# Gate-up with three of eight pairs as seven products, and two sets of sums made again in the down stage

## The chip, the cores and the metric

The kernel runs on one core of a Trainium2 chip. The metric is the device time of one execution in microseconds, as the median of the runs. PE is the matmul engine (PEld its weight loads), DVE the vector engine, ACT the scalar engine, SP the engine that issues the weights' transfers.

## The reference

One layer of a bidirectional encoder on 256 tokens of width 2048, all in float32: a gated feed-forward block, a mixer (a gated recurrence beside windowed attention), and a second gated feed-forward block, each between two RMS norms. The change is in the two feed-forward blocks (FFN):

```python
def swiglu(x, w_gate_up, w_down):
    gate, up = jnp.split(x @ w_gate_up, 2, axis=-1)
    return (jax.nn.silu(gate) * up) @ w_down

ff = swiglu(rms_norm(x, pre_norm_ffn1[layer]), w_ffn1_gate_up[layer], w_ffn1_down[layer])
x = x + 0.5 * rms_norm(ff, post_norm_ffn1[layer])
```

w_gate_up is 2048 x 11264, w_down 5632 x 2048.

## The kernel before

**Products.** A float32 product is made as three: each operand is split into a high part h and a low part l, and h x h, h x l and l x h are added up in PSUM (three, L433 is its matmul). ACT casts the high part and DVE subtracts it from the source for the low part (split_act, L176 and L177). The activations stay on chip with both parts, xt for gate-up and ht for down; the weights are read from memory once, 1 MB at a time, into one of three raw buffers, split in halves of 128 x 1024 and used at once. Five h and five l buffers go round.

**Groups and pairs.** Gate-up runs over 11 groups of 512 gate and 512 up columns. A group has eight pairs of 128-row slices of the inner dimension, and collects 2 x 2 blocks c[m][n] of 128 x 512 in four PSUM banks (m: half of the tokens, n: gate or up). A plain pair takes 2 x 2 x 2 blocks by three products, 24 matmuls. A pair in MIXED_IN takes the seven products of a Strassen-like scheme by three, 21 matmuls (seven). For it DVE forms sums of weight blocks in place in raw (L465, L469, L471) and splits one block of 512 and three halves of 1024, against two halves for a plain pair. Four of the seven products also need sums of the activations: in gate-up these are made once per FFN, while group 0 runs (even), so group 0 is plain. Three are added straight into c, four go to the banks p, which fold adds into c once, in the pair after next from the last seven (L505 to L513); the pairs just around it have their products sorted by bank.

At a group's end, units takes silu(gate) x up out of c (L901 on ACT, L902 on DVE), and after the next group's first pair eight PE transposes (L913) bring the result into two ht tiles. For every second tile up to 18 (MIXED) sums_of then makes the sums (L390, L393, L394), which the down stage uses for its own seven-product pairs.

**Down.** Two runs (Pairs) over 22 ht tiles in the order of a written list, each for 1024 columns. left_sums splits the sums into sp; for tiles in keep it does so once and holds them for the second run. Here begin_next loads and half-splits the plain pair behind a seven ahead of its turn (AHEAD).

A scheduler of the programming layer orders the instructions of each engine when the kernel is built; each engine then runs its list in that order.

Of the kernel before, what the change touches and what calls it, by code (L numbers as in the profile page):

```python
# [11 lines left out]
F32 = mybir.dt.float32  # L12
# [5 lines left out]
ALU = mybir.AluOpType  # L18
# [19 lines left out]
def hymba_layer_kernel(  # L38
# [346 lines left out]

    S3, S1, S2, S4 = range(4)

    def sums_of(u, w):

        nc.vector.tensor_tensor(  # L390
            w[:, 0:2, :], u[:, 0, :].rearrange("p (m t) -> p m t", m=2), u[:, :, P:T], ALU.subtract
        )
        nc.vector.tensor_tensor(w[:, S2, :], w[:, S1, :], u[:, 0, 0:P], ALU.subtract)  # L393
        nc.vector.tensor_tensor(w[:, S4, :], u[:, 1, 0:P], w[:, S2, :], ALU.add)  # L394
        return w

    class Blocks:
# [3 lines left out]

        AHEAD = False
        ahead = None
# [118 lines left out]
        def work(self, upto):  # L522

            while self.pos < upto:
                u = self.order[self.pos]
                if u in self.sums:
                    v = self.order[self.pos + 1]
                    if self.AHEAD and v not in self.sums and self.pos + 1 < upto:
                        self.ahead = [v]
                        self.seven(u, self.begin_next)  # L530
                    else:
                        self.seven(u)
                else:
                    if self.ahead:
                        _, raw, h, l = self.ahead
                        self.ahead = None
                        hs, ls = zip((h, l), split_half(raw, 1))
                    else:
                        hs, ls = split_load(self.source(u))
                    if self.pos == self.after + 1:  # L540
                        self.fold()
                    places = [(k, m, n) for k in range(2) for m in range(2) for n in range(2)]
                    if self.pos in (self.after, self.after + 1):

                        places.sort(key=lambda at: at[1:])
                    for k, m, n in places:
                        self.plain(u, hs, ls, m, n, k)
                self.pos += 1

    class Pairs(Blocks):  # L550
# [4 lines left out]
        HELD = 2  # L555
        AHEAD = True

# [43 lines left out]
        def folded(self):  # L601
            if self.now == 0:
                wide = self.room.tile([P, 2, 512], F32, tag="sp", name=nm("y"), bufs=2)
                y = [
# [198 lines left out]

    MIXED_IN = (2, 4)
    MIXED = range(0, 20, 2)

    def pair_of(xt, u):
# [46 lines left out]
    def ffn(gated, w_dn, post_gain, again, gain=None, lead=None, aside=None):  # L854

        with ExitStack() as st:
# [10 lines left out]
            def sums_room(u):  # L867
                n = MIXED.index(u)
                if n == 0:
                    where_X_was.append(xp.tile([P, 8, 4, P], F32, tag="X", name=nm("sums")))  # L870
                if n < 8:
                    return where_X_was[0][:, n]
                return work.tile([P, 4, P], F32, tag=f"su{n}", name=nm("su"))

            def even(u):
# [5 lines left out]
                if u in MIXED_IN:  # L881
# [3 lines left out]
                    ws = sums_of(whole, room_for("s").rearrange("p (j t) -> p j t", j=4))  # L885
                    w = work.tile([P, 4, 2, P], F32R, tag="sp", name=nm("xs"), bufs=2)
                    split_act(w[:, :, 0, :], w[:, :, 1, :], ws)
# [8 lines left out]
            def units(c, scale):  # L896
# [10 lines left out]
                for j in range(2):  # L907
# [9 lines left out]
                    u = bank.rearrange("p (k t) -> p k t", k=2)  # L917
                    if g in MIXED:
                        u = room_for("z").rearrange("p (k t) -> p k t", k=2)
# [4 lines left out]
                    hts.append(ht)  # L924
                    if g in MIXED:
                        sums[g] = sums_of(u, sums_room(g))
# [26 lines left out]
            ]  # L953
            rows = Pairs(w_dn, orders, hts, sums, work, post_gain, keep=(10, 12, 16))
            rows.half_gain(far["pool"])
            rows.work(1)
            next(waiting)
            rows.first_run()
            rows.work(NU - 4)
# [586 lines left out]
```

## Time and profile before

| | |
|---|---|
| median of 3 runs | 1846.0 us (1845.7 to 1846.99) |
| the profiled execution | 1846.26 us, its span 1844.0 us |
| granted PE clock, mean | 0.998 |
| busy: PE, PEld, DVE, ACT | 99%, 83%, 85%, 59% |
| matmuls | 8670 |
| read from memory | 360 MB, 198 GB/s |

A row of a list of waits has the engine and line that waited, what it waited for, the total in us, how often, and the longest. A row of a timeline has the start in us, how long it took, engine, line, operation, what it writes and reads, shape, count, and in brackets the idle time before it. A row of stretches has the stretch, its length, then each engine's busy us with its count of instructions (PE, PEld, DVE, ACT, POOL), the granted PE clock, the share of time that the DMA engines were busy, and GB/s. A matmul's shown length is that of its whole passage; what it costs is the distance between starts.

### The profile page before, as it was taken

The numbers are of one execution on the slowest core, as the hardware profiler recorded it, in microseconds if no ns is written. First come the engines' busy times: TensorE is split into PE (matmuls) and PEld (weight loads), VectorE is DVE, ScalarE is ACT, GpSimd is POOL, SyncE is SP. The second block draws the span as 40 slices with busy tenths as digits, with TensorE's granted clock in tenths as the row PEclk, the third lists the DMA queues.
The fourth block names the chain that finished last, engine by engine and source line by source line (L and its number), as shares of the span: only waits on it lengthen the run. The fifth ranks groups of instructions, "written<-read, shape, count | busy, mean of one in ns | idle before, by whom it ended". The sixth has DMA issues, their size and how long they took to land.

```text
span 1844.0 us, 23256 instructions
## 1 busy us (share of the span) xinstructions
PE 1832.5 (99%) x8670; PEld 1532.8 (83%) x8670; DVE 1559.4 (85%) x1956; ACT 1078.7 (59%) x1429; POOL 21.4 (1%) x39
## 2 busy tenths in 40 slices
PE   9999999999999999999999999999999999999998
PEld 7888888888888888888888888888888888888886
DVE  7988888888999998477787788888888788899997
ACT  7555555555665666477667656455555555566563
POOL 1000000000000000000000000000000000000000
PEclk9999999999999999999999999999999999999999
DMA  7665655556555565655555456555665556555564
GB/s 254 206 206 184 205 204 184 183 186 203 216 202 211 203 247 208 204 176 158 174 181 154 169 211 223 182 198 193 208 207 193 204 185 206 210 188 188 219 248 155
DMA packets 180880, 365.78 MB, mean 198 GB/s; under 512 B 9256, under 2 KB 56448, under 8 KB 180000
## 3 DMA queue, kind: packets, MB, share of 16 engines
q1 hardware_dynamic: 180416, 364.17, 57.9%
q8 instruction: 68, 1.11, 0.2%
q14 instruction: 44, 0.36, 0.1%
q0 software_dynamic: 352, 0.14, 0.0%
HBM read 360.06 MB, written 4.21 MB: 198 GB/s over the span
## 4 chain that ended last, share of the span: by engine, by line
PE 96%; DVE 1%; ACT 1%; DMA 1%; SPq 0%; issue 0%; DVEq 0%; POOL 0%; ACTq 0%; POOLq 0%
PE pa L433 41%; PE pb L433 38%; PE pa L309 7%; PE pa L314 4%; PE pa L364 1%; PE pa L362 1%; PE pa L363 1%; DMA bias<-row 1%; PE pa L913 1%; PE pb L913 1%; DVE l L177 0%; PE pb L1415 0%; PE pb L1289 0%; PE pb L1267 0%; ACT h L176 0%; PE pb L1351 0%
## 5 line engine op out<-in xcount | busy, mean ns | idle before, releaser
L176 ACT CAST h<-raw 128x1024 fp32r<-128x1024 f32 (+1 forms) x789 | 798.9, 1030 | 635.4 <-PE pb L433 368.5
L177 DVE TENSOR_TENSOR l<-raw,h 128x1024 fp32r<-128x1024 f32 (+1 forms) x789 | 924.7, 1193 | 208.8 <-ACT h L176 175.2
L433 PE MATMUL pa<-h,xt 128*128 128x512 f32 x1248 | 431.0, 391 | 0.1
L433 PE MATMUL pb<-h,xt 128*128 128x512 f32 x1168 | 407.7, 390 | 0.0
L433 PEld LDWEIGHTS pa<-h,xt 128*128 128x128 f32 x1248 | 234.3, 188 | 48.2 <-DVE xt L232 0.6
L433 PEld LDWEIGHTS pb<-h,xt 128*128 128x128 f32 x1168 | 219.3, 188 | 46.0 <-DVE xt L232 0.5
L433 PE MATMUL pa<-l,xt 128*128 128x512 f32 x624 | 243.3, 390 | 0.1
L433 PE MATMUL pb<-l,xt 128*128 128x512 f32 x584 | 227.2, 389 | 0.0
L309 PE MATMUL pa<-xt,h 128*128 128x512 f32 x672 | 164.7, 394 | 0.0
L433 PE MATMUL pb<-h,ht 128*128 128x512 f32 x464 | 162.9, 389 | 0.0
L433 PE MATMUL pa<-h,ht 128*128 128x512 f32 x464 | 162.8, 389 | 0.0
L309 PEld LDWEIGHTS pa<-xt,h 128*128 128x128 f32 x672 | 123.0, 188 | 23.6
L433 PEld LDWEIGHTS pa<-l,xt 128*128 128x128 f32 x624 | 117.3, 188 | 24.3 <-DVE l L177 0.9
L433 PEld LDWEIGHTS pb<-l,xt 128*128 128x128 f32 x584 | 109.7, 188 | 22.6
L465 DVE TENSOR_TENSOR raw<-raw 128x1024 f32<-128x1024 f32 x84 | 102.9, 1224 | 2.2
L433 PEld LDWEIGHTS pb<-h,ht 128*128 128x128 f32 x464 | 87.1, 188 | 18.1
L433 PEld LDWEIGHTS pa<-h,ht 128*128 128x128 f32 x464 | 87.1, 188 | 18.0
L314 PE MATMUL pa<-xt,l 128*128 128x256 f32 x672 | 91.5, 285 | 0.0
L433 PE MATMUL pa<-l,ht 128*128 128x512 f32 x232 | 90.3, 389 | 0.0
L433 PE MATMUL pb<-l,ht 128*128 128x512 f32 x232 | 90.3, 389 | 0.0
L314 PEld LDWEIGHTS pa<-xt,l 128*128 128x128 f32 x672 | 87.1, 191 | 3.2
L433 PE MATMUL pa<-h,sp 128*128 128x512 f32 x176 | 61.3, 389 | 0.0
(280 smaller groups left out, 2134.5 us busy)
## 6 DMA issues: line engine op xcount, KB each, us to landing
raw<-in_w_ffn_gate_up_dram SPq DMA_DIRECT2D x350, 512.0 KB, 4.8
raw<-in_w_ffn_down_dram SPq DMA_DIRECT2D x88, 1024.0 KB, 4.9
raw<-in_w_mix_in_dram SPq DMA_DIRECT2D x52, 1024.0 KB, 5.1
raw<-in_w_mix_out_dram SPq DMA_DIRECT2D x16, 1024.0 KB, 5.3
pg<-in_post_norm_ffn_dram SPq DMA_DIRECT2D x4, 512.0 KB, 5.9
X<-in_x_dram SPq DMA_DIRECT2D x2, 1024.0 KB, 6.9
bias<-row SPq DMA_DIRECT2D x16, 128.0 KB, 4.8
kept<-X SPq DMA_DIRECT2D x2, 1024.0 KB, 4.6
```

What stands on the lines that cost most here:

```text
L176: nc.scalar.copy(hi, src)
L177: nc.vector.tensor_tensor(lo, src, hi.bitcast(F32), ALU.subtract)
L309: nc.tensor.matmul(slot[f], weights(hs, kk, f), xcol(xt, k), start=(k == 0), stop=(k == KT - 1))
L314: nc.tensor.matmul(slot[f][:, 0:T], weights(ls, kk, f), xcol(xt, kh * 8 + kk, 0), start=False, stop=False,)
L362: nc.tensor.matmul(dst, xh, h[:, o : o + n], start=(k == 0), stop=False)
L363: nc.tensor.matmul(dst, xh, l[:, o : o + n], start=False, stop=False)
L364: nc.tensor.matmul(dst, xl, h[:, o : o + n], start=False, stop=(k == KT - 1))
L433: nc.tensor.matmul(self.bank(at), lhs, rhs, start=(n == 1), stop=n in (ends, self.of[at]), skip_group_check=n > ends,)
L465: nc.vector.tensor_tensor(four[:, 0:2], four[:, 0::3], four[:, 1:2].to_broadcast([P, 2, 512]), ALU.add)
L913: nc.tensor.transpose(bank[:, o : o + P], zs[m][:, k * P : (k + 1) * P], ident)
```

## The change

MIXED_IN goes from (2, 4) to (2, 3, 5), so that three pairs of each of the groups 1 to 10 take seven products. The sums of ht tiles 16 and 18 are no longer made in gate-up and kept in tiles of their own; sums_again makes them from ht at the start of down, in another pool, and the freed room holds the third set of gate-up's sums. keep goes from (10, 12, 16) to (16, 18). The flag AHEAD goes: a seven in Gated, too, takes begin_next where its condition holds. The order of the four sums in their tile changes with it (S1 to S4). Lines behind it shift: L465 becomes L464, L902 becomes L913, L506 to L513 become L505 to L512.

```diff
-    S3, S1, S2, S4 = range(4)
+    S2, S3, S4, S1 = range(4)
...
-            w[:, 0:2, :], u[:, 0, :].rearrange("p (m t) -> p m t", m=2), u[:, :, P:T], ALU.subtract
+            w[:, S3::2, :], u[:, 0, :].rearrange("p (m t) -> p m t", m=2), u[:, :, P:T], ALU.subtract
...
                 if u in self.sums:
                     v = self.order[self.pos + 1]
-                    if self.AHEAD and v not in self.sums and self.pos + 1 < upto:
+                    if v not in self.sums and self.pos + 1 < upto:
                         self.ahead = [v]
                         self.seven(u, self.begin_next)
...
-    MIXED_IN = (2, 4)
+    MIXED_IN = (2, 3, 5)
     MIXED = range(0, 20, 2)
+    MIXED_EARLY = MIXED[:8]
...
-                if n < 8:
-                    return where_X_was[0][:, n]
-                return work.tile([P, 4, P], F32, tag=f"su{n}", name=nm("su"))
+                return where_X_was[0][:, n]
+
+            def sums_again(u):
+
+                ht = hts[u].bitcast(F32)
+                w = far["pool"].tile([P, 4, P], F32, tag=f"su{u}", name=nm("su"), bufs=1)
+                nc.vector.tensor_tensor(
+                    w.rearrange("p (k m) t -> p k (m t)", k=2), ht[:, :, 0, :], ht[:, :, 1, :], ALU.add
+                )
+                a11, a21, a12, a22 = (w[:, i, :] for i in range(4))
+                nc.vector.tensor_tensor(a22, a21, a22, ALU.subtract)
+                nc.vector.tensor_tensor(a21, a11, a21, ALU.subtract)
+                nc.vector.tensor_tensor(a11, a22, a11, ALU.subtract)
+                nc.vector.tensor_tensor(a12, a12, a11, ALU.add)
+                return w
...
-                    w = work.tile([P, 4, 2, P], F32R, tag="sp", name=nm("xs"), bufs=2)
+                    w = work.tile([P, 4, 2, P], F32R, tag="sp", name=nm("xs"), bufs=3)
...
-                    if g in MIXED:
+                    if g in MIXED_EARLY:
...
-            rows = Pairs(w_dn, orders, hts, sums, work, post_gain, keep=(10, 12, 16))
+            for u in MIXED[8:]:
+                sums[u] = None
+            rows = Pairs(w_dn, orders, hts, sums, work, post_gain, keep=MIXED[8:])
             rows.half_gain(far["pool"])
             rows.work(1)
             next(waiting)
+            for u in MIXED[8:]:
+                sums[u] = sums_again(u)
             rows.first_run()
```

The scheduler orders the engines anew. On DVE, in the middle of a group before: raw_312 is pair 2 (its last split), raw_325 pair 3, raw_330 pair 4, raw_339 pair 5.

```order
L177 TENSOR_TENSOR l_320_1773<-raw_312_1754,h_319_1772 128x1024
L177 TENSOR_TENSOR l_327_1805<-raw_325_1801,h_326_1804 128x1024
L177 TENSOR_TENSOR l_329_1809<-raw_325_1801,h_328_1808 128x1024
L177 TENSOR_TENSOR l_332_1840<-raw_330_1836,h_331_1839 128x512
L465 TENSOR_TENSOR raw_330_1836<-raw_330_1836 128x1024
L177 TENSOR_TENSOR l_334_1845<-raw_330_1836,h_333_1844 128x1024
L177 TENSOR_TENSOR l_336_1850<-raw_330_1836,h_335_1849 128x1024
L469 TENSOR_TENSOR raw_330_1836<-raw_330_1836 128x512
L471 TENSOR_TENSOR raw_330_1836<-raw_330_1836 128x512
L177 TENSOR_TENSOR l_338_1855<-raw_330_1836,h_337_1854 128x1024
L177 TENSOR_TENSOR l_341_1883<-raw_339_1879,h_340_1882 128x1024
```

The same place now: raw_327 is pair 2 (its last split), raw_340 pair 3, raw_349 pair 4, raw_354 pair 5.

```order
L177 TENSOR_TENSOR l_335_1806<-raw_327_1787,h_334_1805 128x1024
L177 TENSOR_TENSOR l_342_1838<-raw_340_1834,h_341_1837 128x512
L464 TENSOR_TENSOR raw_340_1834<-raw_340_1834 128x1024
L177 TENSOR_TENSOR l_344_1843<-raw_340_1834,h_343_1842 128x1024
L177 TENSOR_TENSOR l_346_1848<-raw_340_1834,h_345_1847 128x1024
L468 TENSOR_TENSOR raw_340_1834<-raw_340_1834 128x512
L470 TENSOR_TENSOR raw_340_1834<-raw_340_1834 128x512
L177 TENSOR_TENSOR l_348_1853<-raw_340_1834,h_347_1852 128x1024
L177 TENSOR_TENSOR l_351_1881<-raw_349_1877,h_350_1880 128x1024
L177 TENSOR_TENSOR l_353_1885<-raw_349_1877,h_352_1884 128x1024
L177 TENSOR_TENSOR l_356_1916<-raw_354_1912,h_355_1915 128x512
```

A seven now follows a seven, and the plain pair 4 stands whole behind pair 3.

On DVE at a group's end before, from the fold's addition into c[1][0]: raw_351 is pair 7, raw_362 and raw_372 are the next group's pairs 0 and 1, raw_377 its pair 2; z and s at L902 are the group's two results.

```order
L511 TENSOR_TENSOR pb_295_1661<-pb_295_1661,z_349_1925 128x512
L510 TENSOR_TENSOR pa_294_1660<-pa_294_1660,s_350_1926 128x512
L177 TENSOR_TENSOR l_355_1968<-raw_351_1960,h_354_1967 128x1024
L512 TENSOR_TENSOR s_350_1926<-pa_322_1777,z_349_1925 128x512
L177 TENSOR_TENSOR l_364_2009<-raw_362_2005,h_363_2008 128x1024
L513 TENSOR_TENSOR pb_296_1662<-pb_296_1662,s_350_1926 128x512
L177 TENSOR_TENSOR l_366_2013<-raw_362_2005,h_365_2012 128x1024
L177 TENSOR_TENSOR l_374_2065<-raw_372_2061,h_373_2064 128x1024
L177 TENSOR_TENSOR l_376_2069<-raw_372_2061,h_375_2068 128x1024
L902 SCALAR_TENSOR_TENSOR z_356_1995<-pa_294_1660,scales_111,z_356_1995 128x512
L902 SCALAR_TENSOR_TENSOR s_357_1998<-pb_296_1662,scales_111,s_357_1998 128x512
L177 TENSOR_TENSOR l_379_2100<-raw_377_2096,h_378_2099 128x512
```

Now, with raw_381, raw_391 and raw_396 as the next group's pairs 0, 1 and 2:

```order
L510 TENSOR_TENSOR pb_310_1694<-pb_310_1694,z_373_2001 128x512
L509 TENSOR_TENSOR pa_309_1693<-pa_309_1693,s_374_2002 128x512
L177 TENSOR_TENSOR l_385_2054<-raw_381_2046,h_384_2053 128x1024
L511 TENSOR_TENSOR s_374_2002<-pa_337_1810,z_373_2001 128x512
L177 TENSOR_TENSOR l_393_2106<-raw_391_2102,h_392_2105 128x1024
L512 TENSOR_TENSOR pb_311_1695<-pb_311_1695,s_374_2002 128x512
L913 SCALAR_TENSOR_TENSOR z_375_2036<-pa_309_1693,scales_111,z_375_2036 128x512
L913 SCALAR_TENSOR_TENSOR s_376_2039<-pb_311_1695,scales_111,s_376_2039 128x512
L177 TENSOR_TENSOR l_395_2110<-raw_391_2102,h_394_2109 128x1024
L177 TENSOR_TENSOR l_398_2141<-raw_396_2137,h_397_2140 128x512
```

The fold has moved from pair 6 to pair 7 of its group: it runs among the next group's splits, and its last addition (L512) stands right in front of the two results. On PE the last products of the group into c[1][1] (pb_311) follow it, behind seven products of the next group (pa_377, pa_378 and one into pb_379):

```order
L432 MATMUL pa_378_2043<-h_382_2049,xt_11_123 128x512
L432 MATMUL pb_379_2044<-h_382_2049,xt_11_123 128x512
L432 MATMUL pb_311_1695<-h_369_1993,xt_12_124 128x512
L432 MATMUL pb_311_1695<-l_370_1994,xt_12_124 128x512
L432 MATMUL pb_311_1695<-h_369_1993,xt_12_124 128x512
L432 MATMUL pb_311_1695<-h_371_1997,xt_12_124 128x512
L432 MATMUL pb_311_1695<-l_372_1998,xt_12_124 128x512
L432 MATMUL pb_311_1695<-h_371_1997,xt_12_124 128x512
L432 MATMUL pb_379_2044<-l_383_2050,xt_11_123 128x512
```

Before, they stood ahead of all of the next group's (pb_296 is c[1][1], pa_358 the next group's c[0][0]):

```order
L433 MATMUL pb_295_1661<-h_354_1967,xt_12_124 128x512
L433 MATMUL pb_296_1662<-h_354_1967,xt_12_124 128x512
L433 MATMUL pb_296_1662<-l_355_1968,xt_12_124 128x512
L433 MATMUL pb_296_1662<-h_354_1967,xt_12_124 128x512
L433 MATMUL pa_358_2001<-h_363_2008,xt_11_123 128x512
```

So the group's second result on DVE now waits for products that come later.

At the start of down DVE had, from the last group's second result on (raw_772 is the first seven of down, sp a set of sums split for it or ahead):

```order
L902 SCALAR_TENSOR_TENSOR s_749_4052<-pb_687_3715,scales_111,s_749_4052 128x512
L177 TENSOR_TENSOR la_775_4156<-raw_772_4151,ha_774_4155 128x512
L177 TENSOR_TENSOR l_777_4161<-raw_772_4151,h_776_4160 128x1024
L465 TENSOR_TENSOR raw_772_4151<-raw_772_4151 128x1024
L177 TENSOR_TENSOR sp_788_4182<-sums_109_681,sp_788_4182 128x4x128
```

and has now (ht_663 and ht_731 are tiles 16 and 18, raw_808 the plain pair in front of that seven):

```order
L913 SCALAR_TENSOR_TENSOR s_788_4129<-pb_724_3790,scales_111,s_788_4129 128x512
L876 TENSOR_TENSOR su_806_4194<-ht_663_3486 128x512
L876 TENSOR_TENSOR su_807_4200<-ht_731_3831 128x512
L880 TENSOR_TENSOR su_806_4194<-su_806_4194 128x128
L880 TENSOR_TENSOR su_807_4200<-su_807_4200 128x128
L881 TENSOR_TENSOR su_806_4194<-su_806_4194 128x128
L881 TENSOR_TENSOR su_807_4200<-su_807_4200 128x128
L882 TENSOR_TENSOR su_806_4194<-su_806_4194 128x128
L882 TENSOR_TENSOR su_807_4200<-su_807_4200 128x128
L883 TENSOR_TENSOR su_806_4194<-su_806_4194 128x128
L883 TENSOR_TENSOR su_807_4200<-su_807_4200 128x128
L177 TENSOR_TENSOR l_812_4213<-raw_808_4206,h_811_4212 128x1024
```

The ten rows of sums_again stand ahead of the second half of that plain pair and of the first seven.

More of the change, by code (lines that the diff above doesn't have):

```diff
@@ L397, in hymba_layer_kernel @@
     class Blocks:
-        AHEAD = False
         ahead = None
@@ L555, in hymba_layer_kernel @@
         HELD = 2
-        AHEAD = True
         def __init__(self, w, orders, tiles, sums, room, gain_src, keep=()):
@@ L602, in folded @@
             if self.now == 0:
-                wide = self.room.tile([P, 2, 512], F32, tag="sp", name=nm("y"), bufs=2)
+                wide = self.room.tile([P, 2, 512], F32, tag="sp", name=nm("y"), bufs=3)
                 y = [
@@ L924, in units @@
                     hts.append(ht)
-                    if g in MIXED:
+                    if g in MIXED_EARLY:
                         sums[g] = sums_of(u, sums_room(g))
```

## The prediction

> **What bounds the kernel now.** I read the page's totals first, then the list of PE's waits, then the busy time of single stretches: the end of group 0, one later gate-up group, and the start of the down stage.
>
> ```profile
> PE 1832.5 (99%) x8670; PEld 1532.8 (83%) x8670; DVE 1559.4 (85%) x1956; ACT 1078.7 (59%) x1429; POOL 21.4 (1%) x39
> ```
>
> ```profile
> PE pb L130 <- DVE idle L124: 1.4, 1, 1.4
> PE pb L1415 <- ACT pt L1407: 0.4, 1, 0.4
> PE pb L210 <- DMA X<-in_x_dram: 0.4, 1, 0.4
> PE pa L210 <- DMA X<-in_x_dram: 0.2, 1, 0.2
> ```
>
> ```profile
> 14.00:58.00 44.00, 44.00 (x207) 35.62 (x205) 39.49 (x71) 30.25 (x61) 2.71 (x5) 1.00 0.64 219
> 185.62:228.67 43.05, 43.05 (x195) 35.75 (x194) 35.77 (x42) 23.01 (x27) 0.00 (x0) 1.00 0.58 196
> 487.00:530.00 43.00, 43.00 (x195) 35.73 (x194) 42.07 (x49) 27.96 (x36) 0.00 (x0) 1.00 0.54 194
> ```
>
> The four waits of PE come to 2.4 us, and none is for a split of weights. In a group (the second stretch; the columns are its length, then the busy time of PE, PEld, DVE and ACT) PE is busy throughout at a granted clock of 1.00, while DVE is busy for 35.77 of 43.05 us and idle for 7.28. The last row says how far this can go: at the start of down DVE is busy for 42.07 of 43.00 us, 98%, and PE still waits for nothing. So PE's count of products sets the time, and DVE may come close to full before PE feels it.
>
> One product's pitch, and that of a transpose, come from PE's timeline of this group:
>
> ```profile
> 191.07 0.27 PE L913 MATMUL pa<-ident,z 128*128 128x128 f32 x1
> ...
> 191.83 0.27 PE L913 MATMUL pb<-ident,s 128*128 128x128 f32 x1
> ...
> 203.06 0.39 PE L433 MATMUL pa<-l,xt 128*128 128x512 f32 x1
> ...
> 205.10 0.39 PE L433 MATMUL pa<-l,xt 128*128 128x512 f32 x1
> ```
>
> The first two rows are the first and the last of eight transposes, 0.76 / 7 = 0.11 us apart. The last two are nine products apart: 2.04 / 9 = 0.2267 us. A group is six plain pairs of 24 products, two of 21, and the transposes: 186 x 0.2267 + 0.89 = 43.05 us, which is the stretch's length. Nothing else is on the path.
>
> **Fewer products.** In each of ten groups per FFN (group 0 stays plain) one more pair takes 21 products in place of 24: 3 x 20 = 60 products, 60 x 0.2267 = 13.6 us less. The Trainium skill ("TensorE: Matmul & The Clock Gate", section "Wait — 56ns, not 53.3ns?") gives N / 2.4 GHz + 2.5 ns for a product at full clock, 215.8 ns for 512 columns. By that the term would be 12.9 us; the trace's 0.2267 decides.
>
> **More work on DVE in a group.** Its durations, from DVE's timeline of the same group, a row of PE's, two of ACT's, and DVE's groups of instructions in this stretch:
>
> ```profile
> 185.33 0.74 DVE L902 SCALAR_TENSOR_TENSOR z<-pa,scales,z 128x512 f32<-128x512 f32 x1
> 185.99 0.74 DVE L902 SCALAR_TENSOR_TENSOR s<-pb,scales,s 128x512 f32<-128x512 f32 x1
> ...
> 201.68 1.23 DVE L465 TENSOR_TENSOR raw<-raw 128x1024 f32<-128x1024 f32 x1
> ...
> 205.24 0.68 DVE L469 TENSOR_TENSOR raw<-raw 128x512 f32<-128x512 f32 x1
> 205.96 0.69 DVE L471 TENSOR_TENSOR raw<-raw 128x512 f32<-128x512 f32 x1
> 207.84 5.82 DVE L177 TENSOR_TENSOR l<-raw,h 128x1024 fp32r<-128x1024 f32 x5 [1.19 <-ACT h L176]
> 213.58 0.69 DVE L506 TENSOR_TENSOR s<-pb,z 128x512 f32<-128x512 f32 x1
> 214.18 0.69 DVE L507 TENSOR_TENSOR pa<-pa,z 128x512 f32<-128x512 f32 x1
> ...
> 217.24 0.69 DVE L511 TENSOR_TENSOR pb<-pb,z 128x512 f32<-128x512 f32 x1
> ...
> 221.30 0.69 DVE L513 TENSOR_TENSOR pb<-pb,s 128x512 f32<-128x512 f32 x1
> ```
>
> ```profile
> 184.71 0.62 PE L433 MATMUL pb<-h,xt 128*128 128x512 f32 x2
> ```
>
> ```profile
> 185.14 0.69 ACT L901 ACTIVATE s<-pb,scales 128x512 f32<-128x512 f32 x1 [0.40 <-PE pb L433]
> ```
>
> ```profile
> 203.01 1.05 ACT L176 CAST h<-raw 128x1024 fp32r<-128x1024 f32 x1 [0.96 <-DVE raw L465]
> ```
>
> ```profile
> L390 DVE TENSOR_TENSOR sums<-z 128x256 f32<-128x256 f32 x1 | 0.4, 418 | 0.0
> L393 DVE TENSOR_TENSOR sums<-sums,z 128x128 f32<-128x128 f32 x1 | 0.3, 282 | 0.0
> ```
>
> By starts, a subtraction of 1024 takes (213.58 - 207.84) / 5 = 1.15, one of 512 takes 0.60, and 0.72 where it waits for the one before it. A seven-product pair has beyond a plain one: one subtraction of 512, one of 1024, an addition of 1024 and two of 512, so 0.60 + 1.15 + 1.15 + 0.60 + 0.60 = 4.1 us. DVE's group becomes 35.8 + 4.1 = 39.9 us of 42.4. Two casts more on ACT (1.05 + 0.6) leave it at 25 of 42 us; no transfer is added, and none moves past another on SP.
>
> The change's words speak of an interleaving. In gate-up it doesn't happen: work is called pair by pair with upto = u + 1, so self.pos + 1 < upto never holds, and DVE's order shows no row of pair 4 inside pair 3. Only down interleaves, as before.
>
> **Whether 39.9 fits into 42.4.** What counts is where DVE must wait. I follow a group by hand from E, the end of PE's last product into c[1][1], which the new order puts behind seven products of the next group.
>
> From E to its use of the low part of pair 3's last half, PE has 17 products left of pair 0, 24 of pair 1, 21 of pair 2, 17 of pair 3, and 8 transposes: 79 x 0.2267 + 0.89 = 18.8 us. DVE's L913 into s begins about 0.2 after E, as L901 does here: the product it waits for has its turn until 184.71 + 0.23 = 184.94, and it begins at 185.14. Then follow, to the same low part: that instruction 0.66; six subtractions of 1024, 6.9; two additions of 1024, the first awaited, 1.27 + 1.15; seven rows of 512, one awaited, 4.3; the three small ones of sums_of at 0.34 + 0.3 + 0.3, by the groups' rows less the overlap; and after L470 a hole, since the cast waits for it and the subtraction for the cast: 0.69 + 0.10 + 1.05 + 0.04, then 1.22. The sum is 18.4. One wait is added: five h buffers go round, and pair 3's first cast (512 wide, 0.6) needs the one that PE gives back at the end of pair 1, at E + 41 x 0.2267 + 0.89 + 0.2 = E + 10.4. Its low part can begin at E + 11.05, and DVE is there at E + 10.7: 0.35. Together 0.2 + 18.4 + 0.35 = 18.95, against 18.8: PE waits for about 0.2 us here, in every group.
>
> The fold is the second place. It now stands at pair 7, the last one. DVE reaches L505 after nine more subtractions of 1024, one of 512 and three additions (10.35 + 0.6 + 2.6), at E + 32.4; PE begins pair 6 (17 + 24 + 21 + 21 + 24 + 21 = 128 products) at E + 0.2 + 128 x 0.2267 + 0.89 = E + 30.1. The fold's rows give 217.24 + 0.69 - 213.58 = 4.35 to the addition into c[1][0] and 221.30 + 0.69 - 213.58 = 8.4 to the one into c[1][1], with one and three plain subtractions between as in the new order: E + 36.8 and E + 40.8. PE needs them 30 products (pair 6 and pair 7's into c[0][0]) and 49 after that start, at E + 36.9 and E + 41.2. Both hold, the first by 0.1. So a group is 42.37 + 0.2 = 42.6 us. Bounds of the wait: 0 (a little slack in any term) to 1.3 (one more cast of 1.05 that nothing covers, plus this 0.2). I take 0.2, the hand sum itself: 20 x 0.2 = 4.0 us.
>
> **Group 0.** It makes a third set of sums: additions of 512 and 256, two of 128, one split of 512, 0.6 + 0.34 + 0.6 + 0.6 = 2.2 us on DVE, once per FFN. The first stretch has DVE busy for 39.5 of 44, so most is covered, but group 1's two sevens follow at once. Bounds 0 and 2.2; I take 0.7, twice 1.4.
>
> **Down.** Two sets of sums are made anew behind the last L913: two additions of 512 and eight small ones in two chains, 2 x 0.6 + 8 x 0.2 = 2.8 us (by L393's full length, 282 ns, 3.5). DVE also comes there with one plain half less done, 1.15. What it has to spare:
>
> ```profile
> 487.37 0.74 DVE L902 SCALAR_TENSOR_TENSOR s<-pb,scales,s 128x512 f32<-128x512 f32 x1
> ...
> 497.44 1.22 DVE L177 TENSOR_TENSOR l<-raw,h 128x1024 fp32r<-128x1024 f32 x1
> ...
> 512.35 1.23 DVE L177 TENSOR_TENSOR l<-raw,h 128x1024 fp32r<-128x1024 f32 x1 [0.16 <-ACT h L176]
> ```
>
> The low part of down's first seven is ready at 498.7. PE reaches it 63 products and 8 transposes after about 487.1: 502.3, 3.6 later. The new order takes 2.8 + 1.15 of that and gives one split of 512 back, 0.6: about 0.3 is left. DVE has no idle time until 512.35, so the pairs behind it run with the same thin lead. Bounds 0 and 2.5 (3.5 + 1.15 - 3.6, and a hole of 1.05 with it); I take 0.7 per FFN, 1.4. In the second half of down one split more (0.6 on DVE, pairs 10 and 12 against 18) lies under PE's products; without that cover it would cost 0.6 per FFN. The sums no longer made in groups 8 and 9 only free DVE.
>
> **Sum.** -13.6 + 4.0 + 1.4 + 1.4 = -6.8. The profiled run took 1846.26 us (span 1844.0 and 2.3 around it), the median is 1846.0. Predicted: 1839.2.
>
> **The rivals.** *DVE sets gate-up's pace.* For: only 2.5 of 42.4 us remain idle on it, a hole of 1.2 at pair 3, 0.35 for a buffer and 0.95 at E (the six products behind L512, less L913 into z) already fill them, and the hole isn't covered. Against: 98% at the start of down without a wait. It decides from 43.05 - 39.9 = 3.15 us of idle per group; with one more uncovered cast a group is 43.5, 20 x 0.45 + 2.8 = +11.8, 1858; if all of today's 7.28 stayed, 47.2 and +83. The Trainium skill ("Perfetto Trace Analysis", section "Identifying the Most-Contended Engine") holds PE's matmul occupancy for no measure of its limit and ranks by weight-load share, which here would put DVE's 85% before PEld's 83% and so predict this rival; the 98% row speaks against it. Chance 0.24.
>
> *Nothing gained.* Waits of 0.5 to 0.7 per group eat the products: within 0.2% of 1846.0, about what a measurement of this kernel can tell from no change (1842.3 to 1849.7). Chance 0.13.
>
> *No wait at all.* Each of my terms is off by a few tenths in favour: -13.6 + 0 to 2.6, so 1832.4 to 1835. Were the interleaving real, pair 4's half would cover the hole and this would be the forecast; as ordered, chance 0.13.
>
> My forecast, 1835 to 1842.3, has 0.50. Slower and "nothing" both lie above it, and below it little: the range goes from 1832 to 1853, leaving out about half of the first rival. Faster 0.63, same 0.13, slower 0.24.
>
> **What would show it.** Right: the groups' stretches at 42.4 to 42.8 us with DVE busy for about 39.9; among PE's waits one for DVE's l at L177, about 0.2 in each group, with 20 to 40 entries; down's start with short waits for l. Wrong: groups at 43 or more; waits of PE for L509, L510 or L512, or for h (the fold or a buffer, not pair 3); the loss outside gate-up; a granted clock below 1.00 behind such waits.

## The result and the profile after

The changed kernel takes 1851.47 us (median of 7 runs, 1851.16 to 1853.58) against 1846.0: a ratio of 1.0032, 95% interval 1.002 to 1.0043. Forecast was 1839.2 with a range of 1832 to 1853. The time lies inside the range, which was drawn wide enough to take in half of a rival, and on the wrong side of no change. Two of the seven runs, 1853.21 and 1853.58, had a mean granted clock of 0.997, the others 0.998 or 0.999. The profiled execution took 1851.47 us with a span of 1849.2, 5.2 more than before.

The shares of the chain that ended last, before:

```profile
PE 96%; DVE 1%; ACT 1%; DMA 1%; SPq 0%; issue 0%; DVEq 0%; POOL 0%; ACTq 0%; POOLq 0%
```

The page's totals and these shares after:

```profile
PE 1829.1 (99%) x8610; PEld 1518.2 (82%) x8610; DVE 1637.6 (89%) x2076; ACT 1102.8 (60%) x1469; POOL 21.4 (1%) x39
...
PE 77%; DVE 16%; ACT 4%; issue 2%; DMA 1%; ACTq 0%; DVEq 0%; POOL 0%; SPq 0%; POOLq 0%
```

The 60 products are gone from PE (8670 to 8610), and yet PE is shown busy for 99%, as before. The chain tells more: a sixth of the span now runs over DVE, where it was 1%. PE's waits (in total, times, longest):

```profile
PE pb L432 <- DVE l L177: 5.1, 20, 0.3
PE pb L432 <- ACT h L176: 2.3, 5, 0.7
PE pa L432 <- ACT h L176: 1.9, 2, 1.0
```

The first row has 20 entries, the number that the prediction asked for, but not where it put them: 18 are at pair 3 of groups 2 to 10, one stands at another place in the first FFN's group 1 and one in the second down stage. Two more rows, 4.2 us together, are new: casts for which PE waits in the two groups 1 and the two down stages. The prediction had named waits for h only as a sign of its being wrong. The same three stretches as before (length, busy time of PE, PEld, DVE, ACT): the end of group 0, one later group, and the start of down.

```profile
14.00:58.00 44.00, 44.00 (x206) 35.66 (x205) 39.66 (x72) 29.40 (x60) 2.72 (x5) 1.00 0.63 222
190.03:232.97 42.94, 42.69 (x193) 35.05 (x192) 39.44 (x47) 24.24 (x29) 0.00 (x0) 1.00 0.57 196
490.70:533.70 43.00, 43.00 (x194) 35.36 (x193) 43.00 (x56) 27.65 (x35) 0.00 (x0) 1.00 0.50 181
```

A group takes 42.94 where 42.6 was forecast. DVE is busy for 39.44 of it, near the 39.9 that were worked out. At the start of down DVE has no idle time left: 43.00 of 43.00, before 42.07. The granted clock is 1.00 in all three.

Where the 5.2 us arise can be read from PE's timeline. A group's result is transposed one pair into the next stage, so the first transpose of a group's result into pa marks the group's end, one pair late; these are those of groups 1 and 10 of each FFN, before:

```profile
104.96 0.27 PE L913 MATMUL pa<-ident,z 128*128 128x128 f32 x1
...
492.44 0.27 PE L913 MATMUL pa<-ident,z 128*128 128x128 f32 x1
...
1226.55 0.27 PE L913 MATMUL pa<-ident,z 128*128 128x128 f32 x1
...
1614.03 0.27 PE L913 MATMUL pa<-ident,z 128*128 128x128 f32 x1
```

and after:

```profile
107.75 0.27 PE L924 MATMUL pa<-ident,z 128*128 128x128 f32 x1
...
494.29 0.27 PE L924 MATMUL pa<-ident,z 128*128 128x128 f32 x1
...
1230.53 0.27 PE L924 MATMUL pa<-ident,z 128*128 128x128 f32 x1
...
1617.13 0.27 PE L924 MATMUL pa<-ident,z 128*128 128x128 f32 x1
```

With the spans these give five stretches. The table has the difference to before in us, for the changed kernel and for five of the experiments told below (their marks are the same transposes). The first row ends behind group 1, and "group 1 to 10" holds groups 2 to 10.

| stretch | changed | e3_two | f3_25 | f1_edges | h3_behind | f2_135 |
|---|---|---|---|---|---|---|
| start to group 1 | +2.8 | -0.1 | +0.3 | 0.0 | +0.1 | -0.2 |
| group 1 to 10, first FFN | -0.9 | 0.0 | 0.0 | +0.4 | -0.7 | -3.8 |
| down, mixer, to group 1 of the second | +2.1 | -0.4 | +2.6 | -0.3 | 0.0 | -0.4 |
| group 1 to 10, second FFN | -0.9 | 0.0 | 0.0 | +0.2 | -0.4 | -3.4 |
| second down and end | +2.1 | 0.0 | +1.0 | 0.0 | +0.4 | +0.4 |

The nine steps from group 1 to 10 should have brought 9 x 0.68 = 6.1 us by products alone and brought 0.9. Here is the place, first in PE's timeline, then in DVE's:

```profile
208.33 0.39 PE L432 MATMUL pb<-h,xt 128*128 128x512 f32 x1
208.96 0.50 PE L432 MATMUL pb<-l,xs 128*128 128x512 f32 x1 [0.25 <-DVE l L177]
209.30 0.39 PE L432 MATMUL pb<-h,xs 128*128 128x512 f32 x1
```

```profile
190.03 0.75 DVE L913 SCALAR_TENSOR_TENSOR s<-pb,scales,s 128x512 f32<-128x512 f32 x1 [1.52 <-PE pb L432]
...
200.80 0.69 DVE L177 TENSOR_TENSOR l<-raw,h 128x512 fp32r<-128x512 f32 x1 [0.48 <-ACT h L176]
...
205.79 0.69 DVE L470 TENSOR_TENSOR raw<-raw 128x512 f32<-128x512 f32 x1
207.69 5.24 DVE L177 TENSOR_TENSOR l<-raw,h 128x1024 fp32r<-128x1024 f32 x5 [1.20 <-ACT h L176]
```

It is the low part of pair 3's last half, in each of groups 2 to 10. The product comes 0.63 after the one before it instead of 0.2267, which is 0.41 late, and the next one starts 0.34 after it, another 0.11. So 0.52 us go here per group, though the list of waits shows 0.25: a product is drawn 0.39 long against a pitch of 0.2267, and what fits between the two counts as busy. On DVE stand the three idle times that the prediction named: for PE at the group's end (1.52; it said 0.95), for the buffer (0.48; it said 0.35) and for the cast behind L470 (1.20, as said).

### The profile page after: what moved, and what is told of

The parts are those of the page before. It is cut to its first block, busy times and chain, and to the rows that moved or that the text cites. A ratio compares the mean times of both kernels' runs of the same rounds, so it can differ in the third digit from the quotient of the medians.

```text
span 1849.2 us, 23410 instructions
## 1 busy us (share of the span) xinstructions
PE 1829.1 (99%) x8610; PEld 1518.2 (82%) x8610; DVE 1637.6 (89%) x2076; ACT 1102.8 (60%) x1469; POOL 21.4 (1%) x39
## 4 chain that ended last, share of the span: by engine, by line
PE 77%; DVE 16%; ACT 4%; issue 2%; DMA 1%; ACTq 0%; DVEq 0%; POOL 0%; SPq 0%; POOLq 0%
PE pa L432 29%; PE pb L432 28%; PE pa L309 8%; DVE l L177 8%; PE pa L314 4%; ACT h L176 4%; DVE raw L464 3%; DVE raw L470 2%; DVE raw L468 1%; PE pa L364 1%; PE pa L363 1%; PE pa L362 1%; DVE sp L177 1%; DVE la L177 1%; PE pa L924 0%
## 5 line engine op out<-in xcount | busy, mean ns | idle before, releaser
L176 ACT CAST h<-raw 128x1024 fp32r<-128x1024 f32 (+1 forms) x829 | 819.3, 1021 | 509.5 <-PE pb L432 149.2
L177 DVE TENSOR_TENSOR l<-raw,h 128x1024 fp32r<-128x1024 f32 (+1 forms) x829 | 955.8, 1181 | 108.5 <-ACT h L176 74.8
L432 PE MATMUL pa<-h,xt 128*128 128x512 f32 x1168 | 406.4, 392 | 0.1
L432 PE MATMUL pb<-h,xt 128*128 128x512 f32 x1048 | 368.5, 390 | 0.1
L432 PEld LDWEIGHTS pa<-h,xt 128*128 128x128 f32 x1168 | 219.3, 188 | 44.8 <-DVE xt L232 0.6
L432 PEld LDWEIGHTS pb<-h,xt 128*128 128x128 f32 x1048 | 196.8, 188 | 41.3 <-DVE xt L232 0.5
L432 PE MATMUL pa<-l,xt 128*128 128x512 f32 x584 | 227.8, 390 | 0.0
L432 PE MATMUL pb<-l,xt 128*128 128x512 f32 x524 | 204.1, 390 | 0.0
L464 DVE TENSOR_TENSOR raw<-raw 128x1024 f32<-128x1024 f32 x104 | 127.1, 1222 | 1.2
L432 PE MATMUL pb<-h,xs 128*128 128x512 f32 x240 | 84.6, 391 | 1.7 <-ACT h L176 1.7
```

The lines of the kernel that those rows point to most:

```text
L176: nc.scalar.copy(hi, src)
L177: nc.vector.tensor_tensor(lo, src, hi.bitcast(F32), ALU.subtract)
L432: nc.tensor.matmul(self.bank(at), lhs, rhs, start=(n == 1), stop=n in (ends, self.of[at]), skip_group_check=n > ends,)
L464: nc.vector.tensor_tensor(four[:, 0:2], four[:, 0::3], four[:, 1:2].to_broadcast([P, 2, 512]), ALU.add)
```

## The experiments

Each was timed in five rounds against the kernel before, on the same chip; only changed lines are shown.

**e2_interleave.**

```diff
-                    if v not in self.sums and self.pos + 1 < upto:
+                    if v not in self.sums and self.pos + 1 < max(upto, self.whole):
+        whole = KT // 2        # in Gated; 0 in Blocks
```

> Edit: in gate-up the interleaving that the change's words announce is made real, so that half a split of pair 4 stands on DVE between the last two additions of pair 3, where DVE now idles for 1.2 us. Theory 1 (a short lead: DVE's chain from the end of the old group to pair 3's last half is too long by 0.4 us, and PE loses 0.5 there in every group): the half of pair 4 is work that is only moved ahead, the hole stays as long for PE or is filled with 1.15 of other work, so PE's wait at pair 3 stays or grows a little unless the cast was what DVE waited for; if the filled hole doesn't delay the last half, the wait stays 0.4 and the total is 1850 to 1853. Theory 2 (the hole itself is lost capacity, and the group is paced by DVE's total of work and holes): filling 1.2 us of it frees 1.2 per group, the wait goes, a group takes 42.4, the total about 1841.

Measured: 1858.69 us, ratio 1.0067 (1.0054 to 1.0079), worse than either theory had it. DVE's timeline says why:

```profile
190.66 0.75 DVE L915 SCALAR_TENSOR_TENSOR s<-pb,scales,s 128x512 f32<-128x512 f32 x1 [1.25 <-PE pb L433]
...
206.54 1.22 DVE L177 TENSOR_TENSOR l<-raw,h 128x1024 fp32r<-128x1024 f32 x1
207.67 0.69 DVE L471 TENSOR_TENSOR raw<-raw 128x512 f32<-128x512 f32 x1
209.55 4.10 DVE L177 TENSOR_TENSOR l<-raw,h 128x1024 fp32r<-128x1024 f32 x4 [1.20 <-ACT h L176]
```

The half of pair 4 stands ahead of the last addition (L471 here), not behind it. The hole is still 1.20 long, and the addition comes 17.01 after L913 into s where it came 15.76 after it in the changed kernel. The hole was not filled, so the run doesn't tell the theories apart; what it shows is that work put ahead of the last addition is paid for.

**e3_two.**

```diff
-    MIXED_IN = (2, 3, 5)
+    MIXED_IN = (2, 4)
```

> Edit: pairs 2 and 4 as seven products as in the kernel before, with the rest of the change kept (two pairs' sums made anew in the down stage, the kept sets, the order of the rows of sums). Theory 1 (the waits come from the third seven of a group, and down lost 1.7 per FFN mainly because DVE arrives there with less lead): 1846 plus 0 to 1.5, so 1846 to 1847.5. Rival (the sums made anew in down cost by themselves): 1846 + 3.4, about 1849.5.

Measured: 1846.24, ratio 1.0 (0.9991 to 1.0009). All stretches are as before. The sums made anew, the other kept sets and the order of the sums cost nothing.

**e7_245.**

```diff
-    MIXED_IN = (2, 3, 5)
+    MIXED_IN = (2, 4, 5)
```

> Edit: the third seven-product pair of a group is pair 4 in place of pair 3 (2, 4 and 5 as seven products), all else as changed. Theory 1 (short lead at pair 3): 4.1 us of DVE's work move from ahead of pair 3's last half to behind it; PE then reaches pair 3 without a wait, and at pair 5, where the low part is ready some 3 us early in the changed kernel, nothing is added; a group takes 42.4, 18 groups gain 0.5 and more, the total is 1840 to 1843. Theory 2 (DVE is full, 39.9 us and its holes fill 42.9): the wait only moves to pair 4 or 5, the total stays 1850 to 1853.

Measured: 1852.22, ratio 1.0033 (1.0021 to 1.0046). Theory 1 missed. Two groups in turn, with the columns as above:

```profile
190.95:233.43 42.48, 42.23 (x191) 34.73 (x190) 39.45 (x46) 24.11 (x29) 0.00 (x0) 1.00 0.59 198
233.43:277.14 43.71, 43.50 (x195) 35.32 (x194) 39.45 (x46) 24.42 (x29) 0.00 (x0) 1.00 0.57 193
```

The stretches differ by 1.23 us at the same DVE work of 39.45, but the second also holds four more PE instructions; by their transposes (192.97, 235.90, 279.15) the two groups take 42.93 and 43.25. In DVE's timeline the second has one more wait for a cast, behind pair 5's last addition:

```profile
258.80 0.69 DVE L470 TENSOR_TENSOR raw<-raw 128x512 f32<-128x512 f32 x1
260.67 5.77 DVE L177 TENSOR_TENSOR l<-raw,h 128x1024 fp32r<-128x1024 f32 x5 [1.17 <-ACT h L176]
```

So moving the third pair back moved PE's wait to pair 5, as theory 2 had it, and one open cast hole more goes with 0.3 us, about half of what three products fewer would bring a group.

**e4_135.**

```diff
-    MIXED_IN = (2, 3, 5)
+    MIXED_IN = (1, 3, 5)
```

> Edit: pairs 1, 3 and 5 as seven products, no two of them neighbours, all else as changed. Theory 1 (short lead): as much of DVE's work stands ahead of pair 3's last half as with 2 and 3, and pair 1's last half is now due at 34 products and 8 transposes after the end of the old group, so PE's wait stays or grows: 1851 to 1858. Rival (two seven-product pairs side by side are the trouble, because the second finds no buffers): the wait goes, a group takes 42.4, the total is about 1841.

Measured: 1849.76, ratio 1.0021 (1.0012 to 1.003), below the theory's range and far above the rival's. A middle group, by its stretch:

```profile
190.50:233.07 42.57, 42.57 (x193) 35.09 (x192) 39.53 (x47) 24.44 (x29) 0.00 (x0) 1.00 0.58 198
```

The groups do reach 42.57, so the theory, by which work ahead of pair 3 is all the same, is wrong. What is gained there goes at the ends, above all in group 1, where PE stands for 2.56 us at one place for a cast:

```profile
69.61 0.79 PE L432 MATMUL pb<-h,xs 128*128 128x512 f32 x1 [2.56 <-ACT h L176]
```

Behind this wait the granted clock (the third number from the end) is 0.50, and products stand about 0.43 us apart in place of 0.2267:

```profile
69.00:75.00 6.00, 5.39 (x13) 3.97 (x14) 5.41 (x6) 3.92 (x5) 0.00 (x0) 0.50 0.43 144
```

From 69.61 to 75.36 PE makes 13 steps, which cost about 2.7 us more than at the full pitch (5.75 - 13 x 0.2267 - 0.11). The first group 1 thus ends 5.5 us later than before (110.50 against 104.96), by the wait and by the clock in about equal parts.

**f1_edges and f2_135.** The third pair is left out in groups 1 and 10, in f1 of pairs 2, 3, 5, in f2 of 1, 3, 5:

```diff
+    JOINS, LEAVES = 3, 5          # f2: 1, 5 and MIXED_IN = (1, 3, 5)
-                if u in MIXED_IN:
+                if u in MIXED_IN and u != JOINS:
+                if g == NG - 1:
+                    del gated.sums[LEAVES]
+                    if g == 1 and u == 3:
+                        summed_tiles(JOINS)
```

> Edit: as changed (pairs 2, 3 and 5), but the third seven-product pair is left out at both ends of each FFN: pair 3 becomes one only from group 2 on (its sums are made in group 1 in place of group 0), and group 10 has pairs 2 and 3 alone. Theory (of the changed kernel's 5.2 us over before, the start lost 3.6 and the two downs 3.4, because DVE enters group 1 and down without a lead; the groups between gain only 0.1 each): the start falls back to before's, the downs too, 4 x 3 products = 2.7 us are given back, of which the waits of 0.5 in the four groups return some: 1844 to 1846.5. Rival (down's and the start's losses are the price of the sums themselves, whatever the lead): 1851.5 + 2.7 - 2, about 1852.

Measured: 1846.84, ratio 1.0004 (0.9995 to 1.0013), 0.3 above the range. The start and both downs are back at before's times (table), so the changed kernel lost at the ends. Groups 2 to 9 gain 0.7 us in the first FFN and 0.9 in the second (by their transposes, 343.7 and 343.6 against 344.4), and group 10, with 2 and 3, takes it back: 44.2 (448.6 to 492.8) against 43.05. PE's waits are nearly all those at pair 3:

```profile
PE pb L432 <- DVE l L177: 4.7, 18, 0.5
```

> Edit: pairs 1, 3 and 5 as seven products, the third left out at both ends (group 1 has 3 and 5, group 10 has 1 and 3). Theory: the groups 2 to 9 take 42.57 as with 1, 3, 5 throughout, because the addition in place of pair 1 fills DVE's wait at the end of a group (0.26 in place of 1.52), so 16 x 0.48 = 7.7 us are gained there, group 1 and the downs are as before: 1838.5 to 1841. Rival (the lead lost at the start comes back in group 2 as it did in group 1): 1842 to 1847.

Measured: 1839.27, ratio 0.9963 (0.9951 to 0.9976), in the theory's range: faster than both kernels, with the same number of products as f1. DVE's timeline at the end of a group, up to pair 3 of the next:

```profile
225.79 1.21 DVE L464 TENSOR_TENSOR raw<-raw 128x1024 f32<-128x1024 f32 x1
227.27 0.75 DVE L917 SCALAR_TENSOR_TENSOR s<-pb,scales,s 128x512 f32<-128x512 f32 x1 [0.27 <-PE pb L432]
...
241.87 0.69 DVE L470 TENSOR_TENSOR raw<-raw 128x512 f32<-128x512 f32 x1
```

Pair 1's addition works in place on raw and stands in DVE's wait for PE, which is 0.27 instead of 1.52. Pair 3's last addition comes 241.87 - 227.27 = 14.60 after L917 into s, 1.16 earlier than the 15.76 of the changed kernel.

**f3_25.**

```diff
-    MIXED_IN = (2, 3, 5)
+    MIXED_IN = (2, 5)
```

> Edit: two seven-product pairs, 2 and 5, so that only the fold moves (from pair 6 to pair 7, with pairs 6 and 7 computed bank by bank to their end), the rest as changed. Theory (it is the third pair's work, not the fold's place, that takes DVE's lead): as before, 1845.5 to 1847. Rival (the late fold holds four of the five h buffers to the end of the group and leaves DVE idle there for 1.5 us): waits in down and at pair 2, 1847.5 to 1850.

Measured: 1849.64, ratio 1.0019 (1.001 to 1.0027); the number is the rival's, though of its waits only those in down came, none at pair 2. The middle groups are exactly as before, and the stretches with the downs lose 2.6 and 1.0 (table), with waits of up to 0.8 on low parts:

```profile
PE pb L432 <- DVE l L177: 1.5, 3, 0.8
```

As e3_two has the same sums and loses nothing, the loss in down comes with the last seven at pair 5 of group 10 and its fold at pair 7, the very end; in f1 and f2 that fold stands at pair 5 and both downs are free. The last seven and its fold move together, so no run tells them apart, and none has them late without the sums made anew. That DVE then enters a down stage in which it is full with less done is argued.

**f4_134.**

```diff
+    JOINS, LEAVES = 1, 4
-    MIXED_IN = (2, 3, 5)
+    MIXED_IN = (1, 3, 4)          # the rest as in f2_135
```

> Edit: as with 1, 3 and 5 and both ends light, but pairs 1, 3 and 4 (group 1 has 3 and 4, group 10 has 1 and 3): the fold goes back to pair 6 and pair 7 gives its first half's buffers back early. Theory (DVE's idle time in a group must be 2.6 us or less): pair 1 still fills the wait at the group's end, but pair 4 asks for its last half while DVE comes from pair 3's, and the fold is due one pair earlier; a group takes 42.4 to 42.8, 1838 to 1845. Rival (buffers held by the late fold are the limit): 42.37, 1837 to 1839.

Measured: 1856.13, ratio 1.0055 (1.0041 to 1.0069); both missed. Pairs 3 and 4 are neighbours, and PE waits for casts:

```profile
PE pb L432 <- ACT h L176: 8.0, 14, 0.8
```

At the group's end DVE stands for a cast, too, in front of both results, where the theory had pair 1 fill its wait:

```profile
228.76 1.83 DVE L177 TENSOR_TENSOR l<-raw,h 128x1024 fp32r<-128x1024 f32 x2 [2.53 <-ACT h L176]
```

**g1_dose_z and g2_dose_s.**

```diff
                     zs.append(z)
+                    if m == 0 and 4 <= len(hts) < 20:      # g2: m == 1
+                        more = stat.tile([P, 512], BF16, tag="jk", name=nm("jk"), bufs=1)
+                        nc.vector.tensor_tensor(more, z, z, ALU.add)
```

> Edit: the changed kernel, and in groups 2 to 9 of each FFN one more addition of 512 on DVE (0.6 to 0.7 us, its result is used by nothing), which reads z and so stands between L913 into z and L913 into s, inside DVE's wait of 1.52 at the end of a group. Theory (what limits a group is the chain on DVE from PE's last product of the old group to pair 3's last half; DVE's wait ahead of that chain is idle time that nothing can use): free, 1851 to 1853. Rival (DVE's work and its waits for casts fill the group, so every further instruction counts): 16 x 0.65 = 10.4 more, about 1862.

Measured: 1853.6, ratio 1.0037 (1.0023 to 1.0051). The addition went into the wait, and the wait shrank by what it took:

```profile
190.99 0.69 DVE L919 TENSOR_TENSOR jk<-z 128x512 bf16<-128x512 f32 x1
192.48 0.75 DVE L913 SCALAR_TENSOR_TENSOR s<-pb,scales,s 128x512 f32<-128x512 f32 x1 [0.80 <-PE pb L432]
```

From group 1 to 10 the time is the changed kernel's within 0.1 us (386.52 against 386.54). The two more in the total lie at the start, ahead of the first group with the addition: 0.8 us had come together by PE's last long wait in group 1 (79.62 against 78.82), of which the cause is open, and 1.6 more follow right behind it, where the granted clock was 0.50:

```profile
80.50:83.50 3.00, 3.00 (x8) 2.33 (x8) 3.00 (x4) 2.43 (x4) 0.00 (x0) 0.50 0.37 94
```

The changed kernel has the same waits there (77.35 and 78.82, shown below), and in its profiled execution the clock stayed at 1.00. So DVE's wait at the group's end is time that costs nothing to fill.

> Edit: the same addition in the same groups, but it reads s and so stands one subtraction behind L913 into s, ahead of pair 2. Theory (the chain): PE's wait at pair 3 grows by all of it, 16 x 0.6 to 0.7, so 9.6 to 11.2 more, 1861 to 1863. Rival (DVE has 2 us to spare in a group wherever they lie): 1851 to 1854.

Measured: 1852.58, ratio 1.0032 (1.002 to 1.0045); the number is the rival's. But more than the dose had changed:

```profile
189.88 0.75 DVE L913 SCALAR_TENSOR_TENSOR s<-pb,scales,s 128x512 f32<-128x512 f32 x1 [1.58 <-PE pb L432]
...
200.69 2.96 DVE L177 TENSOR_TENSOR l<-raw,h 128x1024 fp32r<-128x1024 f32 x3 [1.18 <-ACT h L176]
...
205.55 0.69 DVE L470 TENSOR_TENSOR raw<-raw 128x512 f32<-128x512 f32 x1
206.16 6.51 DVE L177 TENSOR_TENSOR l<-raw,h 128x1024 fp32r<-128x1024 f32 x6
```

The scheduler put a split of pair 3 behind L470 and opened a hole at pair 2 for it, so pair 3's last addition stands at 15.67 after L913, as without the dose (15.76). The run is inconclusive as a dose: what it was to lengthen didn't get longer.

**h1_125 and h2_145.** As f2_135, with pairs 1, 2, 5 and 1, 4, 5:

```diff
+    MIXED_IN = (1, 2, 5)          # h2: (1, 4, 5)
```

> Edit: as with 1, 3 and 5 and light ends, but pairs 1, 2 and 5 (group 1 has 2 and 5, group 10 has 1 and 2). Theory (pair 1's addition fills DVE's wait at the end of a group; nothing else about 1, 3, 5 matters): the wait ahead of L913 into s stays near 0.3, groups at 42.4 to 42.7, 1838.5 to 1841. Rival (two neighbouring pairs are the trouble, and 1, 3, 5 has none): a wait of 0.5 or more at pair 2, groups at 42.9 to 43.2, 1846 to 1849.

Measured: 1863.29, ratio 1.0093 (1.0079 to 1.0107). The wait at the group's end is filled, and yet it is the slowest of all. Both neighbours leave their cast hole open, and pair 5 has a third (1.19 at 216.75), where f2_135 has two holes in a group:

```profile
194.38 1.83 DVE L177 TENSOR_TENSOR l<-raw,h 128x1024 fp32r<-128x1024 f32 x2 [1.20 <-ACT h L176]
...
204.18 6.38 DVE L177 TENSOR_TENSOR l<-raw,h 128x1024 fp32r<-128x1024 f32 x6 [1.17 <-ACT h L176]
```

> Edit: the same with pairs 1, 4 and 5 (group 1 has 4 and 5, group 10 has 1 and 4): the neighbours stand late. Theory (the filled wait alone): groups at 42.4 to 42.7, 1838.5 to 1841. Rival (neighbours): a wait at pair 5, groups at 42.9 to 43.2, 1846 to 1849.

Measured: 1858.26, ratio 1.0066 (1.0052 to 1.008). Both times the rival's direction, beyond its price: with pair 1 and two neighbours, more is lost than the filled wait gives. Neighbours alone don't cost that much: f1_edges has pairs 2 and 3 side by side, its wait unfilled, and takes 1846.84.

**h3_behind.** f2_135 with one instruction of DVE moved:

```diff
+            with tc.issue_after(self.behind) if u == 1 and self.behind else ExitStack():
                 nc.vector.tensor_tensor(
                     four[:, 0:2], four[:, 0::3], four[:, 1:2].to_broadcast([P, 2, 512]), ALU.add
                 )
+                    gated.behind = nc.vector.scalar_tensor_tensor(      # L913 into z and s
```

> Edit: pairs 1, 3 and 5 with light ends as before, with one order on DVE changed: pair 1's addition of 1024 (L464) is queued behind L913 into s, so that it no longer fills DVE's wait at the end of a group. Reading 1 (the filled wait is what 1, 3, 5 gains by): the wait is 1.2 to 1.5 again, all that follows on DVE is 1.15 later, PE waits 0.4 and more at pair 1 or 3, groups at 42.9 to 43.3, 1844 to 1850. Reading 2 (the plain pair between two seven-product pairs is what counts): DVE's lead takes the 1.15, groups stay at 42.4 to 42.7, 1838.5 to 1842.

Measured: 1845.22, ratio 0.9996 (0.9987 to 1.0005), 6 us above f2_135 (the kernel before took 1846.1 beside each); reading 1 holds. DVE waits again, and so does PE, now at pair 1, for a bank that the split of ht gives back:

```profile
185.65 0.75 DVE L919 SCALAR_TENSOR_TENSOR s<-pb,scales,s 128x512 f32<-128x512 f32 x1 [1.39 <-PE pb L433]
186.31 1.22 DVE L466 TENSOR_TENSOR raw<-raw 128x1024 f32<-128x1024 f32 x1
```

```profile
196.63 0.50 PE L433 MATMUL pb<-h,xs 128*128 128x512 f32 x1 [0.23 <-DVE ht L177]
```

A group takes 42.90. One addition of 1.15 us on the wrong side of a wait is thus worth nearly all that the third pair brings; the scheduler moved a few other rows with it, and pair 5's cast hole is even filled here. Spread pairs with the wait unfilled (42.90) do no better than neighbours with it unfilled (f1_edges, 42.92). Of the sets that were run, only the one with both, the filled wait and a plain pair between two seven-product pairs, reaches 42.57. Why the sets with pair 1 and two neighbours (f4, h1, h2) are so much slower isn't settled: h1 and h2 weren't tried with their cast holes covered, and f4 has those of its neighbours covered and is slow all the same.

## Why the prediction was wrong, step by step

Forecast was -6.8 and the profiled span came to +5.2, 12.0 more. By the table 6.8 of this lie in groups 2 to 10 and 5.2 in the rest, the two groups 1 and the two down stages. So two steps failed: the wait at pair 3, sized 0.2 where 0.52 was measured, and the terms for group 0 and down, 2.8 us together where the rest took 5.2 more.

- **Fewer products, -13.6.** Right: 8610 products at the same pitch.
- **DVE's work per group, 39.9 of 42.4.** Right: 39.44 by the stretch. The additions and splits cost what the rows of before said.
- **The wait at pair 3's last half, 0.2 per group.** The right place and the right engine, in 18 of the 20 groups, but a size of 0.52. It was the difference of two sums of 18.8 and 18.95. PE's side came to 208.56 - 189.83 = 18.73 (where the product would have stood, from 0.2 ahead of L913 into s) and DVE's to 208.96 - 189.83 = 19.13; 0.13 of that is the buffer, 0.48 in place of 0.35. DVE's own work, 18.4, was right (208.91, where the low part is ready, less 190.03 and 0.48). Each sum is off by 1% or less, but their difference went from 0.15 to 0.40. The 0.11 that the product behind a wait loses was in no term. The bound of 1.3 held. Together 18 groups took 18 x 0.58 - 12.2 = -1.8 us by the table, not the -8.6 that the prediction's terms give for them.
- **Group 0, +0.7 per FFN.** Too small. By the prediction's terms the start up to the end of group 1 would have taken 0.2 more than before (0.7 + 0.2 of wait - 0.68 of products); it took 2.8 more. In PE's timeline of the changed kernel, group 1 has four waits, all at the seven-product pairs 2 and 3 (xs are the sums):

```profile
72.08 0.50 PE L432 MATMUL pb<-h,xs 128*128 128x512 f32 x1 [0.24 <-ACT h L176]
...
73.34 0.50 PE L432 MATMUL pb<-l,xs 128*128 128x512 f32 x1 [0.24 <-DVE l L177]
...
77.35 0.50 PE L432 MATMUL pa<-h,xs 128*128 128x512 f32 x1 [0.97 <-ACT h L176]
...
78.82 0.50 PE L432 MATMUL pb<-h,xs 128*128 128x512 f32 x1 [0.74 <-ACT h L176]
```

  The prediction counted the sums' 2.2 us and wrote that two sevens follow at once, but didn't walk through group 1. With two pairs in that group, and the third set of sums made there and not in group 0, the loss is gone (f1, f2); which of the two does it wasn't tried.
- **Down, +0.7 per FFN, for sums made anew and half a split less.** Too small, and at the wrong place. The table's third row holds group 1 of the second FFN as well; from group 10's mark to the mixer's first product of L362 (714.46 before, 717.62 after) the first down lost 1.3 us, and the second lost 2.1. It wasn't lost at down's first seven, where the prediction put it, but for the most part at later ones, 56 us (550.11) and 92 us (585.96) behind the mark in the first down. The sums cost nothing with the last seven at pair 4 (e3_two). With it at pair 5 and the fold at pair 7, f3_25 lost 2.2 and 1.1 with only two pairs in a group.
- **The fold at pair 7 costs nothing in a group.** Right (f3_25: groups as before), and yet the fold's place is where the down term should have been looked for: the prediction asked only whether PE waits for the fold, not what DVE has done when the next stage begins.
- **The interleaving doesn't happen in gate-up.** Right by the order; made real it cost 7 us more (e2_interleave).

The rival "nothing gained" named waits of 0.5 to 0.7 per group; that is what the middle groups did. The rival that DVE sets gate-up's pace had the direction right, but not the price of 43.5 a group. DVE sets the pace by its chain of work from the group's end to pair 3, not by its busy time: 0.7 us more of work ahead of this chain was free (g1_dose_z), 1.15 moved out of it brought 6 us (f2_135 against h3_behind). The Trainium skill ("Perfetto Trace Analysis", section "Identifying the Most-Contended Engine") takes PE's matmul occupancy for no good measure of how close PE is to its limit, and judges PE by its weight-load share and by its share of peak FLOP/s, which isn't worked out here. The trace after agrees: PE shows 99% while it loses 0.52 us per group, and DVE's 89% stands before PEld's 82%. It ranked DVE first before the change as well, 85% to 83%, when PE waited for nothing, so the rank alone doesn't say when the limit is reached.

## What to carry to other kernels

An engine that issues in order limits through its waits: count its work between two waits, see where the scheduler put each instruction, and ask of each idle stretch whether work can stand there that needs no free buffer. Try heavy steps with a light one between them: here this paid, though only together with the filled wait. Distrust a term that is the small difference of two large sums. And look at the first and the last round of a loop and at the stage behind it by themselves: here they took more than all the rounds between gave. See also whether the granted clock holds behind a long wait.

## What the runs showed of the hardware

- The product behind one that waited starts 0.34 us after it where the pitch is 0.2267, so each wait of PE costs about 0.11 us more than its length (208.96 to 209.30 in the changed kernel, and 0.34 behind each of the four waits of its group 1).
- A wait shorter than about 0.16 us (0.39 less 0.2267) shows as busy time, and of a longer one that much is missing from the list: 0.41 is listed as 0.25. Groups of f2_135 are 0.2 us longer than their products and transposes, and its list has one wait of 0.2 in all of gate-up.
- The granted clock can fall to 0.50 behind waits of PE of 2.6 us and less. Behind the wait of 2.56 us in e4_135 it was 0.50 over 6.8 us, and in g1_dose_z over 3.4 us behind waits of 0.97 and 0.74 that stand 1.5 us apart; products then start 0.43 us apart in place of 0.2267. The same two waits in the profiled execution of the changed kernel, and one of 1.92 us in e4_135's second FFN, left it at 1.00, so the length of the wait alone doesn't decide it.
